# A two-layer fp32 trunk on one core: order of the weight-split matmuls, small matmuls at the start, norm squares and transposes regrouped

## The chip, the cores and the metric

One core of a Trainium2 chip runs the whole program. The metric is device time in microseconds (us), the median of several executions. The kernel before took 2481.55 us (three executions, 2480.87 to 2482.95).

## The reference

A decoder trunk of two residual layers on one sequence of 256 tokens, width 2048, all in float32. Only the skeleton is shown; rms_norm, rope, softmax and the chunked scan are the usual ones.

```python
for i in range(2):
    hn = rms_norm(h, mixer_norm[i])
    if i == 0:   # differential attention, 8 heads x 2 x 128, value width 256
        mix = diff_attention(hn, w_qkv, ...)    # w_qkv 2048 x 6144, w_o 2048 x 2048
    else:        # Mamba-2 SSD mixer: 8 groups x 8 heads x 64, state 128, conv of 4, SiLU gate
        mix = mamba2_mixer(hn, w_in, ...)       # w_in 2048 x 10304, w_out 4096 x 2048
    h = h + mix
    h = h + square(relu(rms_norm(h, mlp_norm[i]) @ w1[i])) @ w2[i]   # 2048 x 8192, 8192 x 2048
```

## The kernel before

All weights are read from memory once, in units of 128 x 1024 floats (512 KB). A float32 value is multiplied as two parts: ScalarE (ACT) copies the unit to the rounded type fp32r (L151, the high part), and VectorE (DVE) subtracts that from the original (L152, the low part). Activations are split in the same way. A product is then high x high, high x low and low x high, and the low x low term is left out.

There are two ways to multiply. With the weights stationary (`sub_block`, L155), a 128 x 128 square of a weight unit is loaded into TensorE and the activations stream through. The high part of the square meets both parts of the activations, 2 x 256 = 512 columns (L162); the low part meets the activations' high part alone, 256 columns (L163). A unit holds eight such squares, so it gives eight pairs, 512 and 256 columns in turn. Two units (s = 0, 1) make up the 2048 rows of one block of 128 output features. `wide_pair` (L178) makes two blocks together in two PSUM banks: for each s it loads two units, and works through the one and then the other. `wide_one` (L187) makes one block. `wide_pair` serves the query and key projections, the 8 x 5 pairs of blocks of the SSM's input projection (`in_group`, L831), and the first two blocks of each MLP; `wide_one` serves the other blocks of the MLP's first matrix. With the activations stationary (`token_block`, L200) the weights stream, always 512 columns wide (L214, L216); `seven` (L508), which does half of each MLP's first matrix with seven products in place of eight, is 512 wide too (L535 to L537).

Buffers: four tiles for raw units (`raw`), four for split ones (`w`), in PSUM four banks `mm` for the products, three `aux` and one `aux1` for everything else.

Small work lies between the large matmuls. It is written as Python generators (norms, rope, softmax, convolution, scan, transposes), kept in two queues of a `Side` object. `side.tick()` (L68) advances the first generator of each queue to its next `yield`. `sub_block` ticks three times a unit (after squares 2, 5 and 7), `token_block` three times a unit. The Tile framework then orders each engine's instructions: of those that are ready in its own model of time it takes the one that stands earliest in the program. So the order in the program is a priority, not the order on the engine.

The start: for the first four blocks (L287 to L320) the input x and the units of the first four blocks arrive in quarters, each quarter is split and multiplied as it comes, in pairs of 512 and 256 columns (L319, L320), four pairs a quarter and block. The token-major copy of x, `h`, is loaded behind them (L304). Then ACT squares and sums h for the first norm (L321, `norm_square`, L246: two activations of 512 columns for each of four column blocks), copies the four finished banks out (L197), and the value projection begins as a `token_block`, whose first instruction on TensorE needs a weight copy from ACT (L151).

Transposes: `norm_input` (L251) takes the four column blocks of h that a residual has just finished, and for each of two halves makes four transposes into one `aux` bank, splits them into activations (`x_parts`), and yields. `hidden` (L567) does likewise for the MLP's hidden values, four banks one after the other. `av_work` (L398) multiplies the softmax by the values in two halves with a yield behind each (L438, L439). `ssd_work` (L714) multiplies the scan's masks by the inputs, four heads a half group, with a yield behind every second head (L772, L773).

Of the kernel before, what the change touches and what calls it, by code (L numbers as in the profile page):

```python
# [12 lines left out]
F32 = mybir.dt.float32  # L13
# [7 lines left out]
P = 128  # L21
T = 256
# [60 lines left out]
def wait(n):  # L83
    for _ in range(n):
        yield
# [3 lines left out]
def trunk_kernel(ctx: ExitStack, tc: tile.TileContext, x, xt, par, rope, qk, wv, wo, w10, w10s, w20, win, wdt, wout, w11, w11s, w21, out):  # L89
    nc = tc.nc  # L90
    V, S, G, PE = nc.vector, nc.scalar, nc.gpsimd, nc.tensor
# [16 lines left out]
    tri = const.tile([P, P], F32, name="tri")  # L108
    G.affine_select(out=tri, in_=ones, pattern=[[1, P]], compare_op=ALU.is_ge, fill=0.0, base=0, channel_multiplier=-1)

    def aux():
        return ps.tile([P, 512], F32, tag="aux", bufs=3, name="aux")

# [38 lines left out]
            V.tensor_tensor(out=wl[:, s], in0=raw[:, s], in1=wh[:, s].bitcast(F32), op=ALU.subtract)  # L152
        return wh, wl

    def sub_block(w, acts, k0, acc, start, stop):  # L155

        wh, wl = w
        for k in range(8):
            while len(acts) <= k0 + k:
                side.tick()  # L160
            kk = slice(k * P, (k + 1) * P)
            PE.matmul(acc, lhsT=wh[:, kk], rhs=acts[k0 + k], start=(start and k == 0), stop=False)  # L162
            PE.matmul(acc[:, 0, :], lhsT=wl[:, kk], rhs=acts[k0 + k][:, 0, :], start=False, stop=(stop and k == 7))  # L163
            if k in (2, 5, 7):
                side.tick()

    def load(src, n=1):

# [9 lines left out]
    def wide_pair(src, b, acts):  # L178

        pp = [bank() for _ in range(2)]  # L180
        for s in range(2):
            raw = [load(src[b + t, s]) for t in range(2)]
            for t in range(2):
                sub_block(split_weights(raw[t]), acts, 8 * s, pp[t], s == 0, s == 1)
        return pp

    def wide_one(src, b, acts):  # L187
# [63 lines left out]
    def norm_input(j, gain, xs):  # L251

        yield from wait(3)
        for i in range(2):
            ax = aux().rearrange("p (a b) -> p a b", a=2)
            for f in range(2):
                for t in range(2):
                    c = NB * j + T * i + P * f
                    PE.transpose(ax[:, f, t * P:(t + 1) * P], h[:, t, c:c + P], ident)
            xs += x_parts(ax, 2 * j + i, gain)  # L260
            yield
        norm_square(j)

# [26 lines left out]
    with tc.tile_pool(name="xin", bufs=1) as xp:  # L290
        raw, xf = [], []
        for s in range(2):
            pool = (wp, xp)[s]
            raw.append([pool.tile([P, 1024], F32, tag="raw", bufs=4, name="raw") for _ in range(4)])
        for g in range(4):
            for j in range(2):
                xf.append(xp.tile([P, 2, T], F32, tag="xf", bufs=8, name="xf"))
                nc.sync.dma_start(out=xf[-1], in_=x[2 * g + j])
                if j == 0:
                    for b in range(4):  # L300
                        c = slice(512 * (g % 2), 512 * (g % 2 + 1))
                        nc.sync.dma_start(out=raw[g // 2][b][:, c], in_=qk[b, g // 2][:, c])
        for j in range(4):
            nc.sync.dma_start(out=h[:, :, cols(j)], in_=xt[:, :, cols(j)])  # L304
        w = None
        for g in range(4):
            if g % 2 == 0:
                w = [wp.tile([P, 2, 1024], F32R, tag="w", bufs=4, name="w") for _ in range(4)]
            for j in range(2):
                xs += x_parts(xf[2 * g + j], 2 * g + j, C_MIX0)  # L310
            for b in range(4):
                c = slice(512 * (g % 2), 512 * (g % 2 + 1))
                src = raw[g // 2][b][:, c]
                S.copy(out=w[b][:, 0, c], in_=src)
                V.tensor_tensor(out=w[b][:, 1, c], in0=src, in1=w[b][:, 0, c].bitcast(F32), op=ALU.subtract)
                for k in range(4):
                    kk = slice(512 * (g % 2) + k * P, 512 * (g % 2) + (k + 1) * P)
                    act = xs[4 * g + k]
                    PE.matmul(first[b], lhsT=w[b][:, 0, kk], rhs=act, start=(g + k == 0), stop=False)  # L319
                    PE.matmul(first[b][:, 0, :], lhsT=w[b][:, 1, kk], rhs=act[:, 0, :], start=False, stop=(g + k == 6))  # L320
    for j in range(4):  # L321
        norm_square(j)

    with tc.tile_pool(name="att", bufs=1) as ap:
        ident_b = ap.tile([P, P], BF16, name="ident_b")
        V.tensor_copy(out=ident_b, in_=ident)
# [14 lines left out]
        neglam = ap.tile([P, 1], F32, name="neglam")  # L341

        def setup():
            yield from wait(2)
            norm_mean()
            yield from wait(2)
            em = ap.tile([P, 2], F32, name="em")
            V.tensor_scalar_mul(em, ms, EPS)
            rows(epsm, em, "dge")
            yield  # L350
            V.tensor_copy(out=rtok, in_=rsqrt(const, ms, 2, "n"))
            yield
# [45 lines left out]
        def av_work(hd, v, qkn, st, parts_out):  # L398
# [38 lines left out]
            for dv in range(2):  # L437
                PE.matmul(po[:, dv, :], lhsT=v[:, 0, dv * P:(dv + 1) * P], rhs=at[:, 0:T], start=True, stop=False)  # L438
                PE.matmul(po[:, dv, P:T], lhsT=v[:, 1, dv * P:(dv + 1) * P], rhs=at[:, 2 * P:3 * P], start=False, stop=True)  # L439
                yield  # L440
            sq = ap.tile([P, 2, T], F32, tag="on", bufs=1, name="sqo")
            S.activation(sq, po, AF.Square)
            V.tensor_tensor(out=sq[:, 0, :], in0=sq[:, 0, :], in1=sq[:, 1, :], op=ALU.add)
# [113 lines left out]
    def mlp(xs, w1, w1s, w2, pool, after):  # L557
        r2 = const.tile([P, 2], F32, tag="r2", bufs=2, name="r2")
        sas = []

        def sums_of():
            for j in range(KT // 2):
                while len(xs) < 2 * j + 2:
                    yield
                yield from sum_parts(pool, xs[2 * j:2 * j + 2], sas)

        def hidden(u, hid):  # L567
            V.scalar_tensor_tensor(out=u, in0=u, scalar=0.0, in1=u, op0=ALU.max, op1=ALU.mult)
            yield from wait(2)
            uf = u.rearrange("p t a b -> p t (a b)")  # L570
            for j in range(4):
                ax = aux().rearrange("p (a b) -> p a b", a=2)
                for f in range(2):
                    for t in range(2):
                        PE.transpose(ax[:, f, t * P:(t + 1) * P], uf[:, t, T * j + P * f:T * j + P * f + P], ident)  # L575
                hid += split_pair(ax)
                yield

        side.add(sums_of(), slow=True)
        for q in range(4):  # L580
            hid = []
            p7 = None
            wait_for = 2 if q == 0 else 0
            for j in range(8 + wait_for):
                if j >= wait_for:
                    i = j - wait_for
                    while len(sas) <= i:
                        side.tick()
                    if i == 0:
                        p7 = [t for _ in range(3) for t in (bank().rearrange("p a b -> p (a b)"), aux())] + [aux1()]  # L590
                    seven(pool, w1s[q, i], sas[i], p7, i == 0, i == 7)
                    if i == 7:
                        u = seven_out(pool, p7)
                if j < 8:
                    if j % 2 == 0:
                        r = pool.tile([P, 2, T], F32, tag="relu2", bufs=1, name="relu")
                    if q or j > 1:
                        add_sums(r[:, j % 2:j % 2 + 1], [wide_one(w1, 8 * q + j, xs)])
                    elif j == 0:
                        add_sums(r, wide_pair(w1, 0, xs))  # L600
                    if j % 2:
                        if q == 0 and j == 1:
                            norm_mean()
                            V.reciprocal(out=r2, in_=ms)
                        V.scalar_tensor_tensor(out=r, in0=r, scalar=0.0, in1=r, op0=ALU.max, op1=ALU.mult)
                        hid += split_pair(r)
            side.add(hidden(u, hid))
            for j in range(4):
                src = rng(w2, 8 * q + 4, 8 * q + 8) + rng(w2, 8 * q, 8 * q + 4)
                pp = token_block(src, j, hid)  # L610
                for t in range(2):
                    V.scalar_tensor_tensor(out=h[:, t, cols(j)], in0=pp[t], scalar=r2[:, t:t + 1], in1=h[:, t, cols(j)],  # L612
                                           op0=ALU.mult, op1=ALU.add)
                    if q == 3:
                        after(j, t)
# [12 lines left out]
    with tc.tile_pool(name="ssm", bufs=1) as sp:  # L628
# [85 lines left out]
        def ssd_work(g, st, parts_out):  # L714
# [34 lines left out]
            for half in range(2):  # L749
# [19 lines left out]
                for i in range(4):  # L769
# [1 line left out]
                    o = py[64 * (i % 2):64 * (i % 2) + 64, i // 2, :]  # L771
                    PE.matmul(o, lhsT=xdt[:, 0, hd, :], rhs=m0[:, i].rearrange("p a b -> p (a b)"), start=True, stop=False)  # L772
                    PE.matmul(o[:, P:T], lhsT=xdt[:, 1, hd, :], rhs=m1[:, i, :], start=False, stop=True)  # L773
                    if i % 2:
                        yield
                yg = sp.tile([P, 2, T], F32, tag="yg", bufs=2, name="yg")
                for i in range(2):
                    col = C_DS + 4 * g + 2 * half + i
# [192 lines left out]
```

## Time and profile before

| | |
|---|---|
| median of the executions | 2481.55 us |
| profiled execution, its own time | 2480.49 us |
| its span, first to last instruction | 2478.8 us |
| TensorE (PE) busy | 2465.7 us, 99%, 12462 matmuls |
| weight loads (PEld) busy | 2070.7 us, 84% |
| DVE busy | 1968.1 us, 79% |
| ACT busy | 1412.0 us, 57% |
| memory read | 466.88 MB, 189 GB/s over the span |

The busy time of PE counts each matmul from its start to its end, and consecutive ones overlap; the rate is read from the distance between starts. A timeline row that covers several instructions has "x2" or more at its end, and its duration runs from the first one's start to the last one's end.

### The profile page before, as it was taken

How to read it: one execution, taken by the hardware profiler on the slowest of the kernel's cores; microseconds unless marked ns; L12 is line 12 of the kernel's file. 1: busy time of each engine (PE TensorE's matmuls, PEld its weight loads, DVE VectorE, ACT ScalarE, POOL GpSimd, SP SyncE). 2: the span in 40 equal slices, each digit the busy share in tenths (PEclk: the TensorE clock that was granted, in tenths of full speed). 3: DMA queues.
4: the chain of work that ended last, by engine and by line, in shares of the span. 5: the costliest groups of instructions: out<-in, count | busy, mean ns of one | idle time of the engine just before them, and what ended most of it. 6: DMA issues, size and time to landing. Idle time of an engine off the chain costs nothing.

```text
span 2478.8 us, 33082 instructions
## 1 busy us (share of the span) xinstructions
PE 2465.7 (99%) x12462; PEld 2070.7 (84%) x12462; DVE 1968.1 (79%) x2565; ACT 1412.0 (57%) x2014; POOL 1.2 (0%) x8
## 2 busy tenths in 40 slices
PE   8999999999999999999999999999999999999999
PEld 7888888888888888888888888888888888888887
DVE  7888879977958859668886887887997696785874
ACT  7666656545545546556776566675664454554553
POOL 0000000000000000000000000000000000000000
PEclk9999999999999999999999999999999999999999
DMA  7445555465555655556555556455556556555554
GB/s 270 164 156 179 170 182 189 172 235 192 198 195 185 210 182 186 180 182 207 188 187 197 170 191 201 161 187 191 191 204 208 187 183 216 191 199 195 184 186 154
DMA packets 132128, 471.21 MB, mean 190 GB/s; under 512 B 14752, under 2 KB 14944, under 8 KB 131968
## 3 DMA queue, kind: packets, MB, share of 16 engines
q1 hardware_dynamic: 129248, 460.38, 55.2%
q10 hardware_dynamic: 2720, 8.71, 1.1%
q8 instruction: 98, 1.61, 0.3%
q14 instruction: 62, 0.51, 0.1%
HBM read 466.88 MB, written 2.16 MB: 189 GB/s over the span
## 4 chain that ended last, share of the span: by engine, by line
PE 98%; DVE 1%; ACT 0%; DMA 0%; issue 0%; DVEq 0%; SPq 0%
PE pp L214 28%; PE pp L162 26%; PE pp L216 14%; PE pp L163 13%; PE aux L536 2%; PE aux L535 2%; PE aux L537 2%; PE pp L537 2%; PE pp L536 2%; PE pp L535 2%; PE aux L772 1%; PE pp L319 1%; PE aux L575 1%; PE aux L409 0%; PE aux L134 0%; DVE w L522 0%
## 5 line engine op out<-in xcount | busy, mean ns | idle before, releaser
L152 DVE TENSOR_TENSOR w<-raw,w 128x1024 fp32r<-128x1024 f32 x730 | 885.8, 1220 | 333.8 <-ACT w L151 330.5
L151 ACT CAST w<-raw 128x1024 fp32r<-128x1024 f32 x730 | 767.4, 1052 | 571.2 <-PE pp L214 423.2
L162 PE MATMUL pp<-act,w 128*128 128x512 f32 x2768 | 988.9, 400 | 0.1
L214 PE MATMUL pp<-w,act 128*128 128x512 f32 x3072 | 961.0, 392 | 2.3 <-ACT w L151 2.3
L163 PE MATMUL pp<-act,w 128*128 128x256 f32 x2768 | 775.6, 280 | 0.0
L214 PEld LDWEIGHTS pp<-w,act 128*128 128x128 f32 x3072 | 574.4, 188 | 121.6 <-ACT w L151 2.6
L162 PEld LDWEIGHTS pp<-act,w 128*128 128x128 f32 x2768 | 519.9, 188 | 128.1 <-issue 3.6
L216 PE MATMUL pp<-w,act 128*128 128x512 f32 x1536 | 598.6, 390 | 0.0
L163 PEld LDWEIGHTS pp<-act,w 128*128 128x128 f32 x2768 | 522.7, 189 | 4.0 <-DVE w L152 0.4
L521 ACT CAST w<-raw 128x1024 fp32r<-128x1024 f32 (+1 forms) x256 | 241.3, 946 | 200.2 <-PE pp L163 115.9
L216 PEld LDWEIGHTS pp<-w,act 128*128 128x128 f32 x1536 | 288.5, 188 | 57.8
L522 DVE TENSOR_TENSOR w<-raw,w 128x1024 fp32r<-128x1024 f32 (+1 forms) x256 | 272.5, 1086 | 42.4 <-ACT w L521 39.3
L528 DVE TENSOR_TENSOR raw<-raw 128x1024 f32<-128x1024 f32 x64 | 78.0, 1220 | 5.9 <-DMA raw<-in_w11s 2.8
L535 PE MATMUL aux<-w,sa 128*128 128x512 f32 x192 | 75.0, 391 | 0.0
L536 PE MATMUL aux<-w,sa 128*128 128x512 f32 x192 | 74.9, 390 | 0.0
L537 PE MATMUL aux<-w,sa 128*128 128x512 f32 x192 | 74.7, 389 | 0.0
L697 DVE SCALAR_TENSOR_TENSOR cy<-u,cwb,cy 128x256 f32<-128x256 f32 x144 | 63.1, 480 | 1.4
L197 ACT COPY relu<-pp 128x256 f32<-128x256 f32 x64 | 23.9, 373 | 64.3 <-PE pp L163 64.3
L612 DVE SCALAR_TENSOR_TENSOR h<-pp,r,h 128x512 f32<-128x512 f32 x64 | 45.1, 746 | 12.9 <-PE pp L214 12.9
L537 PE MATMUL pp<-w,act 128*128 128x512 f32 x128 | 49.9, 390 | 0.9 <-DVE w L522 0.9
L536 PE MATMUL pp<-w,act 128*128 128x512 f32 x128 | 50.3, 393 | 0.0
L535 PE MATMUL pp<-w,act 128*128 128x512 f32 x128 | 50.1, 392 | 0.0
(228 smaller groups left out, 1905.4 us busy)
## 6 DMA issues: line engine op xcount, KB each, us to landing
raw<-in_w SPq DMA_DIRECT2D x384, 512.0 KB, 3.7
raw<-in_win SPq DMA_DIRECT2D x160, 512.0 KB, 3.3
raw<-in_wout SPq DMA_DIRECT2D x64, 512.0 KB, 3.3
raw<-in_qk SPq DMA_DIRECT2D x56, 512.0 KB, 3.5
raw<-in_w10s SPq DMA_DIRECT2D x32, 768.0 KB, 4.4
raw<-in_w11s SPq DMA_DIRECT2D x32, 768.0 KB, 4.4
raw<-in_wv SPq DMA_DIRECT2D x32, 512.0 KB, 4.0
raw<-in_wo SPq DMA_DIRECT2D x32, 512.0 KB, 3.6
```

Of the source, the lines that this page charges most:

```text
L151: S.copy(out=wh[:, s], in_=raw[:, s])
L152: V.tensor_tensor(out=wl[:, s], in0=raw[:, s], in1=wh[:, s].bitcast(F32), op=ALU.subtract)
L162: PE.matmul(acc, lhsT=wh[:, kk], rhs=acts[k0 + k], start=(start and k == 0), stop=False)
L163: PE.matmul(acc[:, 0, :], lhsT=wl[:, kk], rhs=acts[k0 + k][:, 0, :], start=False, stop=(stop and k == 7))
L214: PE.matmul(pp[t], lhsT=act[:, 0, tok], rhs=m, start=(s + i + k == 0), stop=(s == n - 1 and i + k == 2))
L216: PE.matmul(pp[t], lhsT=act[:, 1, tok], rhs=m, start=False, stop=False)
L521: S.copy(out=w[:, 0], in_=r[:, a:a + n, :])
L522: V.tensor_tensor(out=w[:, 1], in0=r[:, a:a + n, :], in1=w[:, 0].bitcast(F32), op=ALU.subtract)
L528: V.tensor_tensor(out=r[:, 3:5, :], in0=r[:, 0:2, :], in1=bc(r[:, 6, :], 2), op=ALU.subtract)
L535: PE.matmul(pp[n], lhsT=ah, rhs=wh, start=start, stop=False)
L536: PE.matmul(pp[n], lhsT=al, rhs=wh, start=False, stop=False)
L537: PE.matmul(pp[n], lhsT=ah, rhs=wl, start=False, stop=stop)
```

## The change

- `sub_block` is split in two: `sub_part` does either the eight high matmuls of a unit (512 columns each) or its eight low ones (256 each). `sub_block` calls it for the high and then for the low part; `wide_pair` splits both units first, and then does high of the first, high of the second, low of the first, low of the second: 16 matmuls of one width, and 16 of the other. The first four blocks get four and four instead of four pairs.
- The ticks of a unit now come after the fourth and the eighth high matmul and after the last low one.
- 24 matmuls of 128 columns with a tile of ones on both sides, into an otherwise unused use of `aux1`, stand first in TensorE's program. Nothing reads them.
- The norm squares of x move from their place ahead of the copies into the generator `setup`, one column block a tick.
- `norm_input` makes its eight transposes into two banks before it splits the first; `hidden` likewise, two banks at a time; `av_work` has one yield behind both halves; `ssd_work` one behind all four heads.

```diff
+    warm = ps.tile([P, 512], F32, tag="aux1", bufs=1, name="warm")
+    for _ in range(24):
+        PE.matmul(warm[:, 0:P], lhsT=ones_r, rhs=ones_r, start=True, stop=True)
...
-    def sub_block(w, acts, k0, acc, start, stop):
-
-        wh, wl = w
+    def sub_part(w, acts, k0, acc, i, start, stop):
+
         for k in range(8):
             while len(acts) <= k0 + k:
                 side.tick()
-            kk = slice(k * P, (k + 1) * P)
-            PE.matmul(acc, lhsT=wh[:, kk], rhs=acts[k0 + k], start=(start and k == 0), stop=False)
-            PE.matmul(acc[:, 0, :], lhsT=wl[:, kk], rhs=acts[k0 + k][:, 0, :], start=False, stop=(stop and k == 7))
-            if k in (2, 5, 7):
-                side.tick()
+            wk = w[i][:, k * P:(k + 1) * P]
+            if i == 0:
+                PE.matmul(acc, lhsT=wk, rhs=acts[k0 + k], start=(start and k == 0), stop=False)
+                if k % 4 == 3:
+                    side.tick()
+            else:
+                PE.matmul(acc[:, 0, :], lhsT=wk, rhs=acts[k0 + k][:, 0, :], start=False, stop=(stop and k == 7))
+        if i:
+            side.tick()
+
+    def sub_block(w, acts, k0, acc, start, stop):
+        for i in range(2):
+            sub_part(w, acts, k0, acc, i, start, stop)
...
-            for t in range(2):
-                sub_block(split_weights(raw[t]), acts, 8 * s, pp[t], s == 0, s == 1)
+            w = [split_weights(raw[t]) for t in range(2)]
+            for i in range(2):
+                for t in range(2):
+                    sub_part(w[t], acts, 8 * s, pp[t], i, s == 0, s == 1)
...
+        axs = []
         for i in range(2):
             ax = aux().rearrange("p (a b) -> p a b", a=2)
...
-            xs += x_parts(ax, 2 * j + i, gain)
+            axs.append(ax)
+        for i in range(2):
+            xs += x_parts(axs[i], 2 * j + i, gain)
             yield
...
-    for j in range(4):
-        norm_square(j)
-
...
         def setup():
-            yield from wait(2)
+            for j in range(4):
+                yield
+                norm_square(j)
+            yield
             norm_mean()
...
             for dv in range(2):
...
-                yield
+            yield
...
                     PE.matmul(o[:, P:T], lhsT=xdt[:, 1, hd, :], rhs=m1[:, i, :], start=False, stop=True)
-                    if i % 2:
-                        yield
+                yield
```

## Rows read from the trace of the kernel before

**Rows 1.** The page's head: the span and the busy time by engine.
```profile
span 2478.8 us, 33082 instructions
PE 2465.7 (99%) x12462; PEld 2070.7 (84%) x12462; DVE 1968.1 (79%) x2565; ACT 1412.0 (57%) x2014; POOL 1.2 (0%) x8
```

**Rows 2.** Costliest groups: line, engine, shapes, count, busy, mean ns, idle before.
```profile
L162 PE MATMUL pp<-act,w 128*128 128x512 f32 x2768 | 988.9, 400 | 0.1
```

**Rows 3.** Timeline of PE, 999 to 1012 us: start, duration, instruction.
```profile
999.63 0.39 PE L535 MATMUL pp<-w,act 128*128 128x512 f32 x1
...
1003.03 0.39 PE L162 MATMUL pp<-act,w 128*128 128x512 f32 x1
...
1003.60 0.28 PE L163 MATMUL pp<-act,w 128*128 128x256 f32 x1
1003.72 0.40 PE L162 MATMUL pp<-act,w 128*128 128x512 f32 x1
1003.96 0.28 PE L163 MATMUL pp<-act,w 128*128 128x256 f32 x1
...
1008.67 0.40 PE L214 MATMUL pp<-w,act 128*128 128x512 f32 x1
...
1010.06 0.39 PE L214 MATMUL pp<-w,act 128*128 128x512 f32 x1
```

**Rows 4.** Timeline of the weight loads around two 256-wide matmuls of L134.
```profile
1194.33 0.30 PEld L134 LDWEIGHTS aux<-ysr,ones_r 128*128 128x128 f32 x2
1194.56 0.19 PEld L162 LDWEIGHTS pp<-act,w 128*128 128x128 f32 x1
1194.67 0.19 PEld L163 LDWEIGHTS pp<-act,w 128*128 128x128 f32 x1
```

**Rows 5.** DMA issues: tile, tensor, queue, count, size, us to landing.
```profile
raw<-in_win SPq DMA_DIRECT2D x160, 512.0 KB, 3.3
...
raw<-in_qk SPq DMA_DIRECT2D x56, 512.0 KB, 3.5
```

**Rows 6.** Timeline of PE around transposes of the hidden values.
```profile
1011.42 0.60 PE L575 MATMUL aux<-ident,u 128*128 128x128 f32 x4
...
1012.79 0.60 PE L575 MATMUL aux<-ident,u 128*128 128x128 f32 x4
```

**Rows 7.** Timeline of PE around one group of the scan's matmuls.
```profile
1170.51 0.28 PE L163 MATMUL pp<-act,w 128*128 128x256 f32 x1
1170.72 0.66 PE L772 MATMUL aux<-m,xdt 128*64 128x256 f32 x4
...
1171.53 0.50 PE L162 MATMUL pp<-act,w 128*128 128x512 f32 x1
1171.87 0.28 PE L163 MATMUL pp<-act,w 128*128 128x256 f32 x1
```

**Rows 8.** Timeline of PE at the start, with the releaser of the first.
```profile
5.49 0.80 PE L319 MATMUL pp<-act,w 128*128 128x512 f32 x1 [5.49 <-ACT w L314]
...
10.86 0.50 PE L319 MATMUL pp<-act,w 128*128 128x512 f32 x1
```

**Rows 9.** Timeline of PE at the end of the first four blocks.
```profile
30.74 0.28 PE L320 MATMUL pp<-act,w 128*128 128x256 f32 x1
33.33 0.50 PE L214 MATMUL pp<-w,act 128*128 128x512 f32 x1 [2.31 <-ACT w L151]
```

**Rows 10.** Timeline of ACT in the same stretch.
```profile
31.37 0.36 ACT L197 COPY qkn<-pp 128x256 f32<-128x256 f32 x1
...
32.24 1.04 ACT L151 CAST w<-raw 128x1024 fp32r<-128x1024 f32 x1
```

**Rows 11.** Waits, longest first: waiter, releaser, us in total, times, longest.
```profile
ACT w L151 <- PE pp L214: 423.2, 280, 3.7
```

**Rows 12.** Busy time of PE, PEld, DVE, ACT, POOL, clock, DMA, by stretch.
```profile
6.00:8.00 2.00, 2.00 (x7) 1.60 (x7) 1.66 (x4) 1.77 (x4) 0.00 (x0) 1.00 1.05 356
...
1798.00:1860.00 62.00, 62.00 (x317) 52.61 (x316) 60.97 (x76) 37.85 (x47) 0.00 (x0) 1.00 0.60 204
```

More of the change, by code (lines that the diff above doesn't have):

```diff
@@ L315, in trunk_kernel @@
                 V.tensor_tensor(out=w[b][:, 1, c], in0=src, in1=w[b][:, 0, c].bitcast(F32), op=ALU.subtract)
[L316 to L320, printed above, removed]
-    for j in range(4):
-        norm_square(j)
+                for i in range(2):
+                    for k in range(4):
+                        kk = slice(512 * (g % 2) + k * P, 512 * (g % 2) + (k + 1) * P)
+                        act = xs[4 * g + k]
+                        if i == 0:
+                            PE.matmul(first[b], lhsT=w[b][:, 0, kk], rhs=act, start=(g + k == 0), stop=False)
+                        else:
+                            PE.matmul(first[b][:, 0, :], lhsT=w[b][:, 1, kk], rhs=act[:, 0, :], start=False, stop=(g + k == 6))
     with tc.tile_pool(name="att", bufs=1) as ap:
@@ L570, in hidden @@
             uf = u.rearrange("p t a b -> p t (a b)")
[L571 to L576, printed above, removed]
-                yield
+            for j in range(0, 4, 2):
+                axs = []
+                for i in range(2):
+                    ax = aux().rearrange("p (a b) -> p a b", a=2)
+                    for f in range(2):
+                        for t in range(2):
+                            c = T * (j + i) + P * f
+                            PE.transpose(ax[:, f, t * P:(t + 1) * P], uf[:, t, c:c + P], ident)
+                    axs.append(ax)
+                for ax in axs:
+                    hid += split_pair(ax)
+                    yield
         side.add(sums_of(), slow=True)
@@ L773, in ssd_work @@
                     PE.matmul(o[:, P:T], lhsT=xdt[:, 1, hd, :], rhs=m1[:, i, :], start=False, stop=True)
-                    if i % 2:
-                        yield
+                yield
                 yg = sp.tile([P, 2, T], F32, tag="yg", bufs=2, name="yg")
```

## The prediction

> **What bounds the kernel now.** I read the page's head first: PE is busy 99% of the span, DVE 79%, ACT 57% [rows 1]. Busy time alone doesn't prove a bound, so I looked at the idle time before PE's groups: before the 2768 matmuls of L162 it is 0.1 us in all [rows 2]. The waits say the same from the other side: ACT's weight copy waits 423.2 us for PE to give a buffer back [rows 11]. So the time is the sum of the distances between matmul starts, plus what happens before the first one (5.49 us, [rows 8]) and one gap at 30.74 us [rows 9].
>
> The timeline of PE then shows which distances have air in them. Where every matmul is 512 wide, 15 distances fill 999.63 to 1003.03, 3.40 us, so 0.2267 us each [rows 3]. Where 512 and 256 alternate, 16 pairs fill 1003.03 to 1008.67, 5.64 us, so 0.3525 us a pair [rows 3]. At the uniform rate a 256-wide matmul would be half of 0.2267, that is 0.1133, and a pair 0.3400. The alternating stream loses 0.0125 us a pair. Inside it a 256 is followed after 0.12, a 512 after 0.24 [rows 3], so both halves are slower than the uniform stream. After the last 256 the following stream of 512s needs 1.39 us for six distances (1008.67 to 1010.06) where 1.36 would do: 0.03 us is lost once, then the uniform rate holds [rows 3].
>
> **Runs of one width.** Pairs in `wide_pair`: a unit of 512 KB gives eight pairs; 160 units of the SSM projection and 56 of query and key are 1728 pairs [rows 5], and the first two blocks of each MLP, four units each, 64 more: 1792, or 112 sets of 16 pairs. The other 2768 - 1792 = 976 pairs [rows 2] stand in `wide_one`, 122 units of eight.
> - A set of 16 now: 16 x 0.3525 = 5.64. After: 16 x 0.2267 = 3.627, a settling loss of 0.03, and 16 x 0.1133 = 1.813 for the 256s plus what they lose. That loss is not in the trace, for no long run of 256s exists. Its bounds are nothing (they settle at once) and 16 x (0.12 - 0.1133) = 0.11 (they never do). I take 0.02, about the settling loss of the 512s. Sum 5.49, a gain of 0.15; x 112 = 16.8 us (bounds 6.7 to 19).
> - A unit of eight: 2.82 now; 1.814 + 0.03 + 0.907 + 0.015 = 2.766 after, gain 0.054, x 122 = 6.6 us (bounds 2 to 8.5).
> - The first four blocks, runs of four: at most 0.02 a run of the 16, 0.2 us.
> Together 23.6 us, bounds 9 to 28.
>
> By the Trainium skill, "TensorE: Matmul & The Clock Gate", section "Back-to-back issue gap", the distance at full clock is N/2.4 ns plus 2.5 ns, a function of a matmul's own width: 215.8 + 109.2 = 325 ns a pair in any order, and this part would be worth nothing. The trace disagrees on both counts: 226.7 ns for 512, and a 512 in alternation is 0.24 us [rows 3]; the measurement decides.
>
> **Interruptions.** The alternating stream pays nothing extra when small matmuls cut in; a run must settle again, 0.03 us each time. By the code the SSM projections keep six groups for each of eight groups, and the query and key stretches some of their seven a head; a third of the ticks fall at a change of width, where the loss is paid anyway. I take 40 cuts, 1.2 us lost (bounds 0 to 3).
>
> **Groups merged.** Transposes: from one group to the next is 1.37 us (1011.42 to 1012.79), with four matmuls of 0.2267 and four transposes between. The four transposes take 0.60 us with 0.27 of it the tail of the last, so about 0.11 each: 0.907 + 0.44 leaves 0.02 to 0.03 of overhead a group [rows 6]. By the code 24 + 32 groups become 12 + 16, and `av_work` saves 8: 36 x 0.03 = 1.0 us. The scan: from the 256 before a group to the 256 behind the next 512 is 1.36 us, of which the pair's own share is 0.35; the group starts 0.21 behind the 256 (0.12 in the stream), and the 512 behind it takes 0.34 instead of 0.24, so entry and exit cost 0.09 + 0.10 [rows 7]. 32 groups become 16, 16 x 0.19 = 3.0 if the second half of a merged group joins without a gap, none if it pays the same; I take 2.4. Together 3.4 us (bounds 0 to 4).
>
> **Norm squares.** The last matmul of the first blocks starts at 30.74, the next at 33.33, a gap of 2.59 where 0.12 would do: 2.47 lost [rows 9]. The last one ends at 31.02 (30.74 and 0.28), and ACT could copy its bank then; but it is squaring h, copies at 31.37, squares once more, and starts the weight copy at 32.24 [rows 10]. With the squares behind in priority: copy at 31.02, about 0.25 later the weight copy, 1.04 + 0.05 to PE: 32.36, a gain of 1.0. Bounds: 2.47 if the weight copy goes ahead of the bank copies; and a loss of 1.5, if two squares of about 0.75 push in ahead of the next weight copy. The Tile order takes what is ready, so squares whose data are there may fill the same slots as before; the gain is then near 0. I take 1.0. What is late next is the value weights' DMA, queued behind h.
>
> **Small matmuls at the start.** From 5.49 to 10.86 PE does eight pairs in 5.37 us, 0.67 each, against 0.3525 later [rows 3, 8]: nearly half the rate, as at the lower level, 1.2 GHz, although the granted clock reads 1.00 there too [rows 12]. If the 24 matmuls bring the 2.4 GHz level at once, 5.37 - 8 x 0.3525 = 2.55 us are saved. They run in a time in which PE has nothing to do. Taken at 0.11 each at full rate [rows 6] and twice that at half, they last 5.3 us; started after the ones are written, near 1 us, they end by 6.3 at worst, 0.8 late. 256-wide ones at half rate halve that (2.6 us), and a pause of some 2 us before 5.49 then follows, in which the level may fall again. I take 1.0 (bounds -0.8 to 2.55); part can be lost in the ACT chain of the gap above, if that doesn't come earlier too.
>
> **The sum.** 23.6 - 1.2 + 3.4 + 1.0 + 1.0 = 27.8 us off the profiled execution's 2480.5 us (span 2478.8 and 1.7 around it) gives 2452.7. The median of the runs is 1.1 above that execution: 2453.8, so 2454 us.
>
> **What covers the rest.** In `wide_pair` both units are held until their low runs: 4.5 and 5.4 us instead of 2.8. Two of four buffers remain for the next set, and copies of 2 x 1.05 (ACT) and the subtractions of DVE have the 5.5 us of a set to get there, now with the low part needed 3.6 us later than the high one. Queued behind a late copy on ACT is all side work. DVE is the nearest engine: 60.97 of 62 us in the first quarter of the second MLP [rows 12]; a stretch 1% shorter on PE puts it at 99%, so some tenths of a us may stay there.
>
> **The rivals.**
> - *Order does not matter.* The 0.0125 a pair belongs to the 256s wherever they stand. Then only the small parts remain, about 2454 + 23 = 2477. For it: no run of 256s in the trace. Against it: the 512s in alternation are slow as well [rows 3]. Chance 0.06.
> - *Weight loads bound the runs of 256* (slower). A load is 0.19 us long. If loads of a run could not overlap, each 256 would take 0.19 instead of 0.1133: 2768 x (0.19 - 0.126) = +177 us, about 2660. It decides from 0.126 us a 256 (0.3525 - 0.2267). Against it: four loads already start within 0.34 us (1194.33 with x2, 1194.56, 1194.67), 0.113 apart [rows 4]. Chance 0.03.
> - *The held buffers make PE wait* (slower). If a set's first copy could start only once the set before has ended, 1.05 and some 0.2 of signalling stall each of 112 sets: +140 - 28, about 2594. It decides from 0.25 us a set. Against it: ACT's own waits for PE [rows 11]. Chance 0.03.
>
> **How the numbers follow.** The forecast, anything from 2444 (all upper ends but one) to 2468, gets 0.83; a gain that is real but smaller, 2468 to 2476, by runs of 256 that never settle, 0.05. Range for 8 in 10: 2445 to 2469. Faster by over 0.2% (5 us, about what a measurement can tell from no change) is 0.83 + 0.05 + a third of the first rival = 0.90; same 0.04; slower 0.06.
>
> **What would show it.** In the timeline after: 16 distances of 0.227 and then 16 near 0.114 in the query, key and SSM stretches. Idle time before L162's and L163's successors below 1 us in all. The gap behind the first four blocks near 1.5 us, the matmuls of the first stage at 0.23 and 0.11 before 10.86 us. The prediction is wrong if 256s in a run stand 0.12 or more apart, or if PE gets idle time in front of the high run of a set.

## The result

The changed kernel takes 2460.85 us (median of five executions, 2460.63 to 2461.83), the kernel before 2481.14 us in the same comparison: ratio 0.9918, 95% interval 0.9904 to 0.9932. That is 20.3 us, or 0.8%; the forecast was 27.8 us (2454), with 2445 to 2469 as the range.

### The profile page after: what moved, and what is told of

It reads as the page before. It is cut to its first block, busy times and chain, and to the rows that moved or that the text cites. A ratio compares the mean times of both kernels' runs of the same rounds, so it can differ in the third digit from the quotient of the medians.

```text
span 2458.7 us, 33143 instructions
## 1 busy us (share of the span) xinstructions
PE 2452.2 (100%) x12486; PEld 2079.7 (85%) x12486; DVE 1962.1 (80%) x2565; ACT 1406.3 (57%) x2014; POOL 1.2 (0%) x8
## 4 chain that ended last, share of the span: by engine, by line
PE 100%; ACT 0%; DVE 0%; DVEq 0%; issue 0%
PE pp L227 28%; PE pp L166 26%; PE pp L229 14%; PE pp L170 13%; PE aux L554 2%; PE aux L555 2%; PE aux L556 2%; PE pp L555 2%; PE pp L554 2%; PE pp L556 2%; PE aux L796 1%; PE pp L337 1%; PE aux L597 1%; PE aux L428 0%; PE aux L138 0%; PE aux L273 0%
## 5 line engine op out<-in xcount | busy, mean ns | idle before, releaser
L166 PE MATMUL pp<-act,w 128*128 128x512 f32 x2768 | 679.3, 392 | 0.0
L166 PEld LDWEIGHTS pp<-act,w 128*128 128x128 f32 x2768 | 507.2, 188 | 99.8 <-issue 1.0
L170 PEld LDWEIGHTS pp<-act,w 128*128 128x128 f32 x2768 | 362.6, 191 | 17.9 <-issue 0.9
L170 PE MATMUL pp<-act,w 128*128 128x256 f32 x2768 | 373.2, 283 | 0.0
```

What stands on the lines that cost most here:

```text
L166: PE.matmul(acc, lhsT=wk, rhs=acts[k0 + k], start=(start and k == 0), stop=False)
L170: PE.matmul(acc[:, 0, :], lhsT=wk, rhs=acts[k0 + k][:, 0, :], start=False, stop=(stop and k == 7))
```

## The profile after

The head of the page, to set beside [rows 1]: the span is 20.1 us shorter, with 24 matmuls more.

```profile
span 2458.7 us, 33143 instructions
PE 2452.2 (100%) x12486; PEld 2079.7 (85%) x12486; DVE 1962.1 (80%) x2565; ACT 1406.3 (57%) x2014; POOL 1.2 (0%) x8
```

The groups that answer to [rows 2] (L166 does what L162 did, L170 what L163 did). Their busy times can't be compared, since overlapping matmuls of one line now count once; the idle time at the end of each row can, and it is still nothing.

```profile
L166 PE MATMUL pp<-act,w 128*128 128x512 f32 x2768 | 679.3, 392 | 0.0
...
L170 PE MATMUL pp<-act,w 128*128 128x256 f32 x2768 | 373.2, 283 | 0.0
```

The timeline of PE: a set of two blocks in the SSM projection, and one unit of `wide_one` (start, duration, instruction, count; the duration of a merged row ends with its last instruction).

```profile
1167.35 3.82 PE L166 MATMUL pp<-act,w 128*128 128x512 f32 x16
1171.00 2.08 PE L170 MATMUL pp<-act,w 128*128 128x256 f32 x16
1172.91 0.40 PE L166 MATMUL pp<-act,w 128*128 128x512 f32 x1
...
996.73 1.98 PE L166 MATMUL pp<-act,w 128*128 128x512 f32 x8
998.54 1.11 PE L170 MATMUL pp<-act,w 128*128 128x256 f32 x8
999.50 2.00 PE L166 MATMUL pp<-act,w 128*128 128x512 f32 x8
```

The 16 high matmuls fill 3.65 us (1167.35 to 1171.00), 0.228 each: that is as forecast. The 16 low ones fill 1.91 us, 0.119 each and not 0.1133 + a little. The set takes 5.56 us where 16 alternating pairs took 5.64 [rows 3]. The unit of eight shown takes 2.77 (996.73 to 999.50) and the next one, up to 1002.29, 2.79: 2.78 on average instead of 2.82.

The scan's group, now joined, to set beside [rows 7]:

```profile
1162.83 1.07 PE L166 MATMUL pp<-act,w 128*128 128x512 f32 x4
1163.83 0.66 PE L796 MATMUL aux<-m,xdt 128*64 128x256 f32 x4
1164.31 0.39 PE L797 MATMUL aux<-m,xdt 128*64 128x128 f32 x4
1164.53 0.65 PE L796 MATMUL aux<-m,xdt 128*64 128x256 f32 x4
1164.96 0.44 PE L797 MATMUL aux<-m,xdt 128*64 128x128 f32 x4
1165.33 2.18 PE L170 MATMUL pp<-act,w 128*128 128x256 f32 x16
```

Both halves take 1.50 us (1163.83 to 1165.33). Before, one half took 0.81 (1170.72 to 1171.53), so two took 1.62, and entry and exit of 0.19 were paid twice. A joined group saves 0.12 + 0.19 = 0.31 us. The other groups are alike: from the last large matmul to the next, beyond the first one's own distance, each of the 32 half groups takes 0.89 to 0.91 us before, and each of the 16 joined ones 1.59 or 1.60.

The start and the end of the first four blocks, to set beside [rows 8 and 9]:

```profile
1.12 5.38 PE L113 MATMUL warm<-ones_r 128*128 128x128 f32 x24 [1.12 <-DVE ones_r L106]
6.30 3.91 PE L337 MATMUL pp<-act,w 128*128 128x512 f32 x11
10.05 0.64 PE L339 MATMUL pp<-act,w 128*128 128x256 f32 x4
...
30.52 0.49 PE L138 MATMUL aux<-sqr,ones_r 128*128 128x512 f32 x1 [0.19 <-ACT sqr L132]
31.25 0.50 PE L138 MATMUL aux<-sqr,ones_r 128*128 128x512 f32 x1 [0.23 <-DVE sqr L133]
32.35 0.51 PE L227 MATMUL pp<-w,act 128*128 128x512 f32 x1 [0.60 <-ACT w L155]
```

The small matmuls last until 6.30, so the first real one comes 0.8 us later than before. The value projection begins at 32.35 instead of 33.33. The gap looks smaller in the last column than it is: two sums of a query norm, work that came later before, now stand inside it.

And ACT in that gap, to set beside [rows 10]: a square of h (L262) still stands between the last bank copy and the weight copy.

```profile
30.37 0.38 ACT L210 COPY qkn<-pp 128x256 f32<-128x256 f32 x1
30.63 0.64 ACT L262 ACTIVATE junk<-h 128x512 bf16<-128x512 f32 x1
...
31.26 1.04 ACT L155 CAST w<-raw 128x1024 fp32r<-128x1024 f32 x1
```

## The experiments

**One part at a time.** Four kernels, each the kernel before with one part of the change.

```diff
 # e1_runs: sub_part, wide_pair and the first four blocks as in the change
+            for i in range(2):
+                for t in range(2):
+                    sub_part(w[t], acts, 8 * s, pp[t], i, s == 0, s == 1)
 # e2_merges: norm_input, hidden, av_work and ssd_work as in the change
-                    if i % 2:
-                        yield
+                yield
 # e3_norms: norm_square moved into setup()
 # e4_small: the 24 small matmuls
```

> The kernel before with only the runs of one width (sub_part, wide_pair, the first four blocks). Theory: each matmul of fp32r costs its columns at 2.4 GHz plus a fixed 13.3 ns, so a 256 in a run costs 0.120 us and not 0.1133; a set of 16 pairs takes 5.57 us instead of 5.64 and a unit of eight 2.78 instead of 2.82, in all 112 x 0.074 + 122 x 0.04 = 13 us: about 2468 us. Rival: the runs are worth the predicted 23 us or close to it by themselves, and another part of the change costs some of it: below 2462 us. Second rival: the runs are cut by the small groups so often that by themselves they bring under 6 us: above 2475 us.

> The kernel before with only the merged groups (norm_input, hidden, av_work, ssd_work). Theory: 28 groups of transposes and 8 of av_work fewer at 0.03 us and 16 groups of the scan fewer at 0.15 to 0.19: 3.5 to 4 us, about 2477 us, with two groups of eight scan records joined in the timeline. Rival: in an alternating stream a small group costs nothing but its own work, as no run has to settle again, and a joined scan group pays the same between its halves: no gain, 2481 us.

> The kernel before with only the norm squares of x moved into the generator. Theory: the Tile order puts them into the same free slots of ACT whatever their place, so the gap behind the first four blocks stays near 2.3 to 2.6 us and the time within 0.5 us of before. Rival, as predicted: the gap falls to near 1.5 us and the time by 1 us.

> The kernel before with only the 24 small matmuls at the start. Theory: each takes 0.213 us at the lower level, they end at 6.3 us and put the first real matmul 0.8 us later, while the full rate comes 1.9 us earlier; the first four blocks end 0.2 to 0.6 us earlier, the time falls by that or less. Rival: the earlier full rate is worth its 1 to 2.5 us.

| | median us | ratio to before, 95% interval | us off 2481.37 |
|---|---|---|---|
| runs alone | 2471.95 | 0.9962, 0.9950 to 0.9974 | -9.4 |
| merged groups alone | 2482.05 | 1.0003, 0.9994 to 1.0011 | +0.7 |
| norm squares alone | 2480.33 | 0.9995, 0.9987 to 1.0004 | -1.0 |
| small matmuls alone | 2480.66 | 0.9998, 0.9989 to 1.0006 | -0.7 |

The sum is -10.5 us, and the whole change is -20.3. Half of the gain belongs to no single part. The expectation for the runs (-13) was too high and that for the merged groups (-3.5 to -4) wrong, by the same cause: waits. The waits of PE in the merged groups alone (waiter, releaser, total us, times, longest):

```profile
PE pp L163 <- DVE w L152: 7.6, 5, 1.5
```

The timeline of PE around one of them:

```profile
1201.75 0.59 PE L737 MATMUL aux<-bc 128*128 128x256 f32 x2
1202.18 0.38 PE L738 MATMUL aux<-bc 128*128 128x128 f32 x2
1204.11 0.39 PE L163 MATMUL pp<-act,w 128*128 128x256 f32 x1 [1.54 <-DVE w L152]
```

And of DVE at that time:

```profile
1199.65 1.67 DVE L816 SCALAR_TENSOR_TENSOR yg<-yg,pa,rs_c 128x256 f32<-128x256 f32 x4
1201.23 0.48 DVE L705 SCALAR_TENSOR_TENSOR cy<-u,cwb,cy 128x256 f32<-128x256 f32 x1
1201.63 1.29 DVE L232 TENSOR_TENSOR act<-yg,act 128x512 fp32r<-128x512 f32 x2
1202.83 1.22 DVE L152 TENSOR_TENSOR w<-raw,w 128x1024 fp32r<-128x1024 f32 x1
```

With fewer yields, a group's norm work (L816, L232) falls into the same stretch as the convolution (L705), and DVE gets to the subtraction of a weight unit (L152) only at 1202.83. In the alternating order the low part is needed one matmul after the high one, so PE stands still until 1204.11. Such waits take back what the joined groups save: the eight groups of L737 and L738 cost 13.4 us in all, against 4.6 for the same groups of the kernel before. The runs alone have five waits in a milder form, at a run of 256. PE's waits in that kernel:

```profile
PE pp L166 <- DVE w L152: 1.2, 5, 0.2
```

And PE's timeline at one of them:

```profile
1203.94 1.11 PE L166 MATMUL pp<-act,w 128*128 128x256 f32 x8
1205.28 0.98 PE L166 MATMUL pp<-act,w 128*128 128x256 f32 x6 [0.23 <-DVE w L152]
```

The second row starts 1.34 us behind the first, where eight distances of 0.12 are 0.96, and its own six take 0.10 longer than such six do (0.98 against 0.88): nearly 0.5 each, 2.5 us in all. A sixth wait, for an activation (L162 on DVE's L251, 0.4 us), delays by 0.7. With these 3.2 us the 9.4 of the runs alone become 12.6, near the 13 expected. There the low part is needed a whole run of 512s later, and DVE is still late, but by less. The runs alone move the ticks too, and no run tells whether these waits come from the order or from the ticks.

**Two parts together.** `e6_runs_merges` is the kernel before with the runs and the merged groups.

> The kernel before with the runs and the merged groups, without the small matmuls and the moved norm squares. By themselves the two were worth -9.4 and +0.7 us. Theory: the merged scan groups save 5 us of PE in both, but alone they make DVE late for the low parts at five places (1.8 us each); with runs a low part is needed 3.6 us after its high part and the lateness is hidden; and the five waits of 0.4 us of the runs alone go too: about 2463 us, -18. Rival: the effects add, -9 us, 2472.

2463.17 us, ratio 0.9923 (0.9910 to 0.9937): -18.4 us, as the theory had it and twice the sum. Among PE's waits neither of the two above is left; the start and the gap behind the first blocks are all there is:

```profile
PE pp L333 <- ACT w L326: 5.7, 2, 5.6
PE pp L223 <- ACT w L151: 2.1, 1, 2.1
```

**Which of the merged groups.** `e7_scan_split` is the changed kernel with the scan's yield as before.

```diff
-                yield
+                    if i % 2:
+                        yield
```

> The changed kernel with the scan's yield behind every second head put back; the transposes and av_work stay merged. Theory: of the merges only the scan's is worth anything, 0.32 us for each of 16 groups: +5 us, 2466, and up to 2 us more if the waits of the runs alone come back. Rival: the merged transposes carry the saving, then within 1.5 us of the changed kernel.

2469.51 us, 8.7 above the changed kernel. 16 x 0.31 = 5.0 of it is the groups' own time. The waits of the runs alone are back among PE's:

```profile
PE pp L170 <- DVE w L156: 1.2, 5, 0.2
PE pp L166 <- DVE act L255: 0.6, 1, 0.6
```

The five of the first row, 1.2 us together, delay by 0.5 each as in the runs alone, 2.5 us; the one of the second row delays by 0.9 with the distance behind it. That makes 8.4 of the 8.7. So the scan's yield alone brings the waits back, and the other merged groups don't keep them away. For the transposes no run shows a gain by itself; the overhead of 0.03 a group [rows 6] was within what the rows can tell.

**What a matmul costs.** `e5_widths` puts a measuring series in place of the 24 small matmuls; only its distances are read.

```diff
+        widths = [512] * 60 + [384] * 40 + [320] * 40 + [256] * 40 + [128] * 40 + [512, 256] * 20 + [512, 384] * 20 + [512] * 20
+        for i, n in enumerate(widths):
+            k = P * (i % 4)
+            PE.matmul(warm[:, 0:n], lhsT=wide[:, k:k + P], rhs=wide[:, 0:n], start=True, stop=True)
```

> The changed kernel with a measuring series in place of the 24 small matmuls: 60 matmuls of 512 columns, 40 each of 384, 320, 256 and 128, then 512 and 256 in turn, 512 and 384 in turn, and 20 of 512, all fp32r ones; only distances between starts are read. Theory A, a fixed cost per matmul: N/2.4 + 13.3 ns, so 226.7, 173.3, 146.7, 120.0. Theory B, as the prediction took it, a rate (distance in proportion to the columns): 226.7, 170.0, 141.7, 113.3. Theory C, a rate, but no weight load in less than 0.120 us: 226.7, 170.0, 141.7, 120.0. In turn: 512 above 230 after any change of width under A with settling.

The timeline merges a stretch into one row. Two rows with the same start, from a short and a long window, give the distance: the difference of durations by the difference of counts. In order: 512, 384, 320, 256, then 512 and 256 in turn, then 512 and 384 in turn (these rows show the first one's width).

```profile
7.77 1.52 PE L118 MATMUL warm<-wide 128*128 128x512 f32 x6
7.77 8.55 PE L118 MATMUL warm<-wide 128*128 128x512 f32 x37
17.72 1.56 PE L118 MATMUL warm<-wide 128*128 128x384 f32 x8
17.72 5.54 PE L118 MATMUL warm<-wide 128*128 128x384 f32 x31
24.81 1.48 PE L118 MATMUL warm<-wide 128*128 128x320 f32 x9
24.81 4.42 PE L118 MATMUL warm<-wide 128*128 128x320 f32 x29
30.73 1.48 PE L118 MATMUL warm<-wide 128*128 128x256 f32 x11
30.73 3.52 PE L118 MATMUL warm<-wide 128*128 128x256 f32 x28
...
39.61 1.78 PE L118 MATMUL warm<-wide 128*128 128x512 f32 x9
39.61 5.59 PE L118 MATMUL warm<-wide 128*128 128x512 f32 x31
46.67 1.64 PE L118 MATMUL warm<-wide 128*128 128x512 f32 x7
46.67 6.60 PE L118 MATMUL warm<-wide 128*128 128x512 f32 x31
```

7.03/31 = 0.2268, 3.98/23 = 0.1730, 2.94/20 = 0.147, 2.04/17 = 0.120. Theory A, N/2.4 + 13.3 ns, gives 226.7, 173.3, 146.7 and 120.0; a rate (B) would have given 170.0 and 141.7 in the middle, and so would a floor under the weight loads (C). So 13.3 ns are paid for each matmul of 256 to 512 columns. In turn, 3.81/22 = 0.1732 is 0.346 a pair of 512 and 256: here turning costs nothing beyond the fixed part, while in the kernel before a pair took 0.3525 [rows 3]. But 512 and 384 in turn take 4.96/24 = 0.2067, 0.413 a pair where A gives 0.400, so turning can cost in this series too. What makes the difference of 6 ns was the question of the next run.

**What pairs lose in turn.** `e12_turns` put 512 and 256 in turn five times, with the same and with changing operands, with a sum carried on and without.

> The changed kernel with a second measuring series in place of the 24 small matmuls: 512 and 256 columns in turn, 24 pairs each time, behind a run of one width: (1) same moving tile, each matmul its own sum, behind 512s; (2) the same behind 256s; (3) as (1) but all into one sum; (4) as (1) with four moving tiles in turn; (5) one sum, four moving tiles, and the 256s with weights from another half, as in the kernel. The first series gave 347 ns a pair, no more than N/2.4 + 13.3 for each, where the kernel before took 352.5. Theory: what the pairs lose is how the reads of the operands fall, so (4) and (5) lose 4 to 7 ns a pair and (1) to (3) none. Rival 1: it is the sum that is carried on, then (3) and (5) lose. Rival 2: it is where the pairs start, then (1) behind 512s loses too and (2) differs from it.

It doesn't answer the question: the whole run went at another clock (span and mean granted clock of the core). At it runs of 512 stood 0.251 us apart and the pairs of all five series 0.376, which is 512 and 768 columns at 0.851 x 2.4 GHz: neither the fixed part nor a loss is there to be compared.

```profile
core 0: 2766.9 us, clock 0.851
```

**The gap and the start.** `e8_h_later` loads h behind the first value weights; `e9_no_small` leaves out the 24 small matmuls; `e10_short` has 19 of them.

```diff
 # e8_h_later: the four loads move from the first stage into setup()
+            for j in range(4):
+                nc.sync.dma_start(out=h[:, :, cols(j)], in_=xt[:, :, cols(j)])
             for j in range(4):
                 yield
                 norm_square(j)
```

> The changed kernel with the load of h put behind the first value weights in the program, so that the norm squares have no data yet when ACT copies the first banks. Theory: the weight copy then goes ahead of the squares, the gap of 2.3 us behind the first four blocks falls to 0.5 to 1.4 us: -1 to -1.8 us, 2459.5. Rival: the squares land in the next copies' way and PE waits there for as long: no change, or up to +2 us.

> The changed kernel without the 24 small matmuls. Theory: they put the first real matmul at 6.3 us instead of 5.5 and bring the full rate at 9 instead of 10.9 us; the first four blocks end 0.3 to 0.8 us later without them, 2461.5 us. Rival: the delay costs as much as the rate brings, no difference.

> The changed kernel with 19 small matmuls instead of 24. Theory: at 0.213 us each they end at 5.2 us, in time for the first real one at 5.5; the full rate comes no later, and the first four blocks end up to 0.8 us earlier: about 2460.2 us. Rival: the end of the first four blocks is set by DVE's and ACT's splits of the first quarters, or by the gap behind them, and nothing changes.

2460.39 us (0.9916, 0.9902 to 0.9929), 2461.07 (0.9922, 0.9908 to 0.9935) and 2461.27 (0.9920, 0.9906 to 0.9933): no difference from the changed kernel's 2460.85 that these runs can tell. With h later the first weight copy did go ahead of the squares, and the next one came behind them: the value projection starts at 30.65 instead of 32.35, PE waits again at 34.72 (0.69 us for a weight copy), and the projection's 17th matmul stands at 35.75 instead of 36.14. Of the 1.7 us gained 0.4 are left. Without the small matmuls the first real one starts at 5.73, but the low level lasts longer:

```profile
5.73 4.73 PE L333 MATMUL pp<-act,w 128*128 128x512 f32 x11 [5.73 <-ACT w L326]
10.30 0.63 PE L335 MATMUL pp<-act,w 128*128 128x256 f32 x4
```

The same eleven high matmuls take 4.57 us to the first low one (5.73 to 10.30), against 3.75 with the small matmuls (6.30 to 10.05). 0.8 us gained by the rate, 0.6 lost by the later start: the rival of the expectation. These are single executions; in that of `e8_h_later`, with the same 24 small matmuls, the eleven take 4.23 us, so the gain by the rate is 0.3 to 0.8.

**Longer runs for single blocks.** `e11_one_runs` gives `wide_one` runs of 16 as well.

```diff
+        w = [split_weights(raw[s]) for s in range(2)]
+        for i in range(2):
+            for s in range(2):
+                sub_part(w[s], acts, 8 * s, pp, i, s == 0 and i == 0, s == 1 and i == 1)
```

> The changed kernel with runs of 16 in wide_one too (high of both units, then low of both). Theory: a change to 512 costs 24 ns over its first five distances and the start of a run of 256 gives 8 ns back, so 61 changes fewer save 61 x 0.016 = 1 us: 2459.8 us, if no wait for the split buffers appears, as two units are held where seven of the products need three more of the four tiles. Rival: those waits appear, slower by 2 us or more, above 2463.

2459.50 us (2459.19 to 2460.09; ratio 0.9913, 0.9900 to 0.9927). It is the fastest of all, by 1.35 us at the medians, and near what the theory said; the intervals of the two ratios overlap, so by the times the step is likely and not proven. The traces show it: what the distances between L166's and L170's matmuls have above N/2.4 + 13.3 ns falls by 1.0 us. No wait for buffers stands among PE's.

## Why the prediction was right

The time fell inside the range and the cause was the one named, but two terms were off in opposite directions, and a third was not seen at all. From the starts of all matmuls in the two traces, the 20.1 us between the spans divide into 12.5 in the runs of `sub_block`, 5.4 at the small groups and the distance behind each, 1.2 in the other streams (0.9 of it one wait of L537 for DVE that is gone) and 1.0 before the value projection. The runs brought 11 us less than forecast; groups and waits made up for about 4 of these, which was not foreseen. So that the sum came as near as it did is in part luck.

- **Runs of one width: 23.6 us forecast, about 13 measured.** By the rows, 112 x (5.64 - 5.56) + 122 x (2.82 - 2.78) = 9.0 + 4.9 = 13.9. Summed over the two traces, from the value projection on and without the first distance behind a small group, what the distances behind `sub_block`'s matmuls have above N/2.4 + 13.3 ns fell from 15.7 to 3.3 us, 12.5. The step that failed is "a 256-wide matmul would be half of 0.2267, that is 0.1133". A distance of 0.2267 holds 13.3 ns that do not shrink with the width, so a 256 in a run costs 0.120, the upper bound of the prediction's own range (0.12). The prediction's reading that in alternation "both halves are slower" is wrong as well: there a 256 was followed after 0.117 on average, sooner than in a run (0.120), and a 512 after 0.238 instead of 0.227, so the whole loss stood behind the 512s. The settling loss of the 512s, 0.03 a change, was right (0.027 over the first five distances).
- **Groups merged: 3.4 us forecast; 5.0 measured for the scan, no gain shown for the transposes.** The two halves join with less than no gap: 16 x 0.31 where 16 x 0.15 was taken.
- **Interruptions: 1.2 us lost by the forecast.** No such loss shows: the first distance behind a small group has 0.08 us too much before (14.8 us behind 193 groups) and 0.07 after (10.6 behind 148), so at this distance a run pays no more for a cut than the alternating stream did. What settling follows in a run is within the 12.5 above.
- **Waits: none forecast.** The paragraph on what covers the rest looked at ACT's copies and at how busy DVE is, while PE hardly waits behind the first gap (once before, 0.9 us at L537, and not at all after), and so missed that DVE's order decides when a low part is there. Alone, the joined groups cost five waits of 1.5 us and the runs five that delay by 0.5; together both vanish. That the runs need a low part 3.6 us later is in the prediction, as a cover; that another part of the change would need this cover is not. The experiment with both parts shows the cover; which yields bring DVE's work together I read from one timeline only.
- **Norm squares: 1.0 us forecast.** The value projection starts 0.98 us earlier, yet the order on ACT is as before: a square still stands ahead of the weight copy. The earlier start comes in part from the first stage, which ends 0.7 us earlier. Moved alone, the squares gave 1.0 us with an interval that reaches no difference. The prediction's doubt, that ready squares fill the same slots, describes what the trace shows.
- **Small matmuls: 1.0 us forecast, nothing that can be told.** "End by 6.3 at worst, 0.8 late" is what happened: each of the 24 took 0.213 us, near the 0.22 that the prediction took. The later start gives back most of what the rate brings; between the traces with and without them 0.2 us are left, from the value projection to the end.
- **The rivals.** Order did matter; the first rival is out by the runs alone (-9.4 us). Weight loads did not bound the runs: the 256s stand 0.120 apart, below the 0.126 from which that rival decides, and theory C fails at 384 and 320. PE did not wait for the held buffers: no such wait is in the list of the changed kernel.
- **The prediction's own signs.** It called itself wrong "if 256s in a run stand 0.12 or more apart". They stand 0.119 apart in the row shown and 0.120 over all of them, so on this step its own sign is against it. Of the others, no idle time in front of the runs came true, and the gap did not shrink to 1.5 us: from the last 256 of the first blocks (30.05) to the value projection it is 2.3, with two sums inside.

## What to carry to other kernels

Take the cost of a matmul from two widths, not from one: with a fixed part in it, halving the width does not halve the time, and the gain of regrouping is smaller than the slope suggests. Ask of each part of a change what slack it needs and which other part makes it; here joined groups were worth nothing until the order of the matmuls gave the subtraction 3.6 us of room. A gain at the start that only moves where an engine waits is paid back at the next wait: with h later, 0.4 of 1.7 us were left.

## What the hardware showed that was not expected

- A fixed 13.3 ns for each fp32r matmul of 256 to 512 columns at full clock, beside the columns at 2.4 GHz. At a lower clock it does not show: in the stretch with a granted clock of 0.50 below, a 512 is followed after 0.427 us, which is its columns at 1.2 GHz, and at the granted clock of 0.851 above the columns account for everything too. 128 columns do not follow it either: in `e5_widths` they stand 0.112 apart at a granted clock of 1.00 (3.51 - 1.50 us for 18 more, from 34.73 on), where N/2.4 + 13.3 ns would be 0.067, and the 24 small matmuls stand 0.213 apart. Each has a weight load of its own, and no run tells whether the load or the moving columns set this.
- After the gap behind the first four blocks TensorE can fall back to its lower level. In the kernel with only the norm squares moved, the 512s from 33.80 on stand 0.43 us apart for 3 us (timeline of PE):

```profile
33.80 0.63 PE L214 MATMUL pp<-w,act 128*128 128x512 f32 x1
34.23 0.63 PE L216 MATMUL pp<-w,act 128*128 128x512 f32 x1
```

  Busy time of PE, PEld, DVE, ACT and POOL, granted clock, DMA share and GB/s of that stretch:

```profile
33.80:36.80 3.00, 3.00 (x9) 2.31 (x8) 2.59 (x6) 2.92 (x8) 0.00 (x0) 0.50 0.57 176
```

  The granted clock is 0.50 there, the 1.2 GHz level, after 2.5 us with only two sums on the engine; eight distances of 0.43 in place of 0.23 lose 1.6 us. The profiles of `e4_small` (from 34.18) and `e6_runs_merges` (from 34.53) have the same fall, those of the kernel before and of the changed kernel, with like gaps, do not. The mean granted clock of an execution reads 0.999 in those three and 1.000 in these two; it read 0.999 in 21 of the 29 executions of the kernel before that stand beside the first four experiments, in 3 of 11 with the norm squares moved (2481.2 us on average, against 2479.9 for the other eight), and in none of the changed kernel's five. So part of what moving the squares is worth may be that the fall comes less often; no run isolates this, and what brings it about stays open.
- Turning between 512 and 256 columns loses 6 ns a pair in the kernel and none in a series with equal operands, while 512 and 384 in turn lose 13 ns a pair in that same series. The cause stays open.
